# The recurrent branch's output weights read whole ahead of attention, and small DMAs issued by GpSimd

## Chip, cores and metric

The kernel runs on one core of one Trainium2 chip. The metric is device time of one execution in microseconds (us); lower is better. Times below are medians over runs; the trace is of one profiled execution. Engines: TensorE (PE, with its weight loads PEld), VectorE (DVE), ScalarE (ACT), GpSimd (POOL), SyncE (SP). An ending q (ACTq, SPq, POOLq) marks DMA issues by that engine's sequencer.

## The reference

One layer of a hybrid block on 1024 tokens of width 1024, in float32. An input projection feeds three dilated-window attentions (12 heads), a recurrent branch (RWKV, 8 heads of 64) and two gates; both branches are projected to the model's width, gated and added; an output projection and a mixture of 32 experts follow.

```python
h = rms_norm(x, norm1_gain)
p = h @ w_in
q, k, v, p_rwkv, p_gate = jnp.split(p, [...], axis=-1)
...
for g, (win, dil) in enumerate(ATT_PATTERNS):
    o_g, l_g = dilated_window_attention(q[:, :, g], k[:, :, g], v[:, :, g], ..., win, dil)
...
wts = jax.nn.softmax(jnp.stack(lses, axis=0), axis=0)
att = jnp.einsum('gbsh,gbshe->bshe', wts, jnp.stack(outs, axis=0).astype(jnp.float32))
y_att = att.reshape(B, S, ATT_OUT_WIDTH).astype(x.dtype) @ w_att_out
y_rwkv = rwkv7_time_mix(p_rwkv, ..., w_rwkv_out)          # ends with o @ w_rwkv_out
gates = jax.nn.sigmoid(p_gate.astype(jnp.float32)).astype(x.dtype)
mixed = gates[..., :D] * y_att + gates[..., D:] * y_rwkv
x = x + mixed @ w_out
x = x + hierarchical_moe(rms_norm(x, norm2_gain), ...)    # 32 experts, 2 per token
```

## The kernel before

Every float32 product is made of three fp32r matmuls: an operand is split into a high part (ACT copies it to fp32r) and a low part (DVE subtracts), by `split`, and `mm3` adds high x high, high x low and low x high in PSUM. The stages follow one another: input projection and RWKV preparation (0 to 410 us of the trace), the RWKV scan (to about 550), attention (about 573 to 921), the two branch projections (to 1022), output projection and router (to 1140), experts (1160 to the end). In the scan and in attention the remaining input-projection matmuls (line L307) fill PE; the last of them end at 932.

The order on each engine is set by a scheduler when the kernel is built: it takes the code's order, but moves an instruction according to when its operands and its buffer are free. Buffers come from pools; a pool opened where a closed one lay gets its memory when the last user of the old one is done. A DMA is issued by the engine it is written for and waits in that engine's queue, ahead of what stands behind it: for its source, for its buffer, and for the previous transfer that used the same one of eight completion semaphores of its kind (DMAHW for ACT and SP, DMASW for POOL).

The branch stage. `ohi`/`olo` are the split recurrent output. `load_wr(n)` reads a 128-column slice of `w_rwkv_out` (256 KB, rows of 512 bytes) and splits it into `wrh`/`wrl`; for each n two PSUM tiles are made with 12 matmuls each (L1090 through `mm3`), gated with `ga` into `mix`. Beside it 4 MB of `w_out` are read and split (`woh`, `wol`) for the later output projection. `MLc` holds the maxima and sums of the three windows' softmaxes; 12 small instructions turn them into mixing weights `wgt`, which are stored to `dWG` and read back broadcast over 64 partitions (`wb`, 256 KB each, 12 loads). For each of two head pairs three window outputs `og` are multiplied with `wb` and added; the third product is POOL's (L1187). The sums are split into `ahi`/`alo`, the attention output weights `w_att_out` are read by SP in two tiles and split, and 96 matmuls, gated with 16 more `ga` tiles, are added to `mix`.

The output projection. `mixsplit(i)` splits the 128 tokens `mix[:, i]` into `mxh` and a low part; the first two are written ahead of the loop, and the scheduler sets their place. Their `mxh` come from the pool `pmx`. Constants for norm and router (`g2`, `wr36`, `g2c`, `br36`, `rc`) are loaded on ACT's queue, and a block of zeros, `zpad`, is stored to the output's spare rows. Expert weights (512 KB pieces) are prefetched by SP into a list of areas; the first five are the pool `mr2`, then six of `mr`, then parts of `mix`.

```python
    for i in range(NRAW2):
        load_raw(N0 + i)
    ...
    def mixsplit(i):
        mh = pmx.tile([128, 8, 128], F32R, name="mxh")
        if i < 2:
            ml = raw4k().bitcast(F32R).rearrange("q (n t) -> q n t", t=128)
        ...
        split(mh, ml, mix[:, i])
```

## Time and profile before

| | before |
|---|---|
| median of 3 runs | 1787.5 us |
| lowest, highest | 1787.35, 1788.68 us |
| span of the profiled execution | 1787.2 us |
| own time of the profiled execution | not recorded beside the span |
| mean granted TensorE clock | 0.968 |
| PE, DVE, ACT, POOL busy | 94%, 71%, 49%, 26% of the span |
| DMA | 363.44 MB, mean 203 GB/s |

The span runs from the first to the last instruction. Shares are means over stages with different limits; for the change only the stretch from 920 to 1040 us matters directly, and the rows further down are of it and of two stretches used for prices.

### The profile page before, as it was taken

The page shows a single profiled execution, that of the slowest core. Times are in us where ns is not written, and L with a number is a line of the kernel's source. Part 1 is how long each engine was busy: PE and PEld are TensorE (multiplying, and loading weights), DVE is VectorE, ACT ScalarE, POOL GpSimd, SP SyncE. Part 2 cuts the span into 40 slices and gives each one's busy share as a digit, 9 for nine tenths or more (in the row PEclk, how much of TensorE's full clock was granted, in tenths as well). Part 3 has the DMA queues.
Part 4 walks back from the last instruction along what each step waited for, and adds up shares of the span by engine and source line. Part 5 has one row for each costly group of instructions (what it writes and reads, how often), then busy time and mean ns, then how long its engine had stood idle before and what let it go on. Part 6 is the DMA issues. An engine that isn't in the chain of part 4 may idle for free. (4 is left out here: it accounts for less than half of the span.)

```text
span 1787.2 us, 25862 instructions
## 1 busy us (share of the span) xinstructions
PE 1680.3 (94%) x9395; PEld 1325.3 (74%) x9396; DVE 1263.4 (71%) x2122; ACT 873.7 (49%) x1315; POOL 461.6 (26%) x380
## 2 busy tenths in 40 slices
PE   8999999999999999999998999699998999899996
PEld 6677777777777777777766777588777877777884
DVE  5647788783664444444436666689999999999985
ACT  4523434422221333344342122388777888777774
POOL 0110112223431000000100311234455455444431
PEclk9998989998999999999999999799999999999998
DMA  8323223363662110111249773699999999999991
GB/s 285 138 69 133 92 92 116 136 241 119 219 198 80 33 45 30 48 40 51 101 145 259 220 288 130 220 307 362 358 349 309 378 343 382 356 354 360 373 348 28
DMA packets 145619, 363.44 MB, mean 203 GB/s; under 512 B 17316, under 2 KB 62772, under 8 KB 145484
## 3 DMA queue, kind: packets, MB, share of 16 engines
q1 hardware_dynamic: 123108, 303.67, 47.4%
q0 software_dynamic: 15872, 50.35, 10.1%
q10 hardware_dynamic: 6504, 7.69, 1.6%
q8 instruction: 76, 1.25, 0.3%
q14 instruction: 59, 0.48, 0.1%
HBM read 307.49 MB, written 62.29 MB: 207 GB/s over the span
## 5 line engine op out<-in xcount | busy, mean ns | idle before, releaser
L1531 PE MATMUL pb<-u,xTh 128*128 128x512 f32 x1024 | 338.4, 406 | 1.2 <-ACT xTh L1526 1.2
L307 PE MATMUL pa<-xlo,wh 128*128 128x512 f32 x736 | 307.7, 418 | 0.0
L307 PE MATMUL pa<-xhi,wl 128*128 128x512 f32 x736 | 302.1, 411 | 2.3 <-DVE wl L278 2.3
L307 PE MATMUL pa<-xhi,wh 128*128 128x512 f32 x736 | 301.7, 410 | 1.5 <-DVE raw L427 1.0
L1417 DVE TENSOR_TENSOR u<-raw,u 128x1024 fp32r<-128x1024 f32 x182 | 297.5, 1676 | 5.5 <-ACT u L1415 5.3
L1415 ACT ACTIVATE u<-raw 128x1024 fp32r<-128x1024 f32 x216 | 224.3, 1056 | 47.5 <-PE pb L1531 28.8
L1531 PE MATMUL pb<-u,xTl 128*128 128x512 f32 x512 | 209.2, 409 | 21.1 <-DVE xTl L1527 21.1
L1531 PEld LDWEIGHTS pb<-u,xTh 128*128 128x128 f32 x1024 | 191.3, 189 | 40.7 <-ACT xTh L1526 2.0
L307 PEld LDWEIGHTS pa<-xlo,wh 128*128 128x128 f32 x736 | 141.1, 192 | 40.6 <-issue 11.0
L307 PEld LDWEIGHTS pa<-xhi,wh 128*128 128x128 f32 x736 | 141.4, 192 | 34.5 <-issue 2.9
L307 PEld LDWEIGHTS pa<-xhi,wl 128*128 128x128 f32 x736 | 141.6, 192 | 34.1 <-DVE wl L278 3.2
L1417 DVE TENSOR_TENSOR u<-mix,u 128x1024 fp32r<-128x1024 f32 x108 | 162.2, 1538 | 4.4 <-ACT u L1415 4.4
L1531 PE MATMUL pa<-u,hTh 128*128 128x512 f32 x512 | 146.0, 406 | 5.5 <-POOL u L1417 4.6
L1415 ACT ACTIVATE u<-mix 128x1024 fp32r<-128x1024 f32 x128 | 133.6, 1057 | 23.1 <-PE pb L1531 15.8
L1531 PEld LDWEIGHTS pb<-u,xTl 128*128 128x128 f32 x512 | 96.8, 189 | 45.0 <-DVE xTl L1527 27.9
L978 DVE SCALAR_TENSOR_TENSOR Sb<-pb,rqk,bias 128x128 f32<-128x128 f32 (+1 forms) x96 | 35.5, 406 | 124.5 <-PE pb L977 116.6
L1510 POOL DMA_INDIRECT out<-row,tba x30 | 62.6, 2086 | 219.4 <-ACT u L1415 56.5
L1531 PEld LDWEIGHTS pa<-u,hTh 128*128 128x128 f32 x512 | 94.6, 191 | 28.2 <-POOL u L1417 5.5
L1417 POOL TENSOR_TENSOR u<-raw,u 128x1024 fp32r<-128x1024 f32 x34 | 101.3, 2980 | 47.2 <-ACT u L1415 41.6
L276 ACT ACTIVATE wh<-wr 128x1024 fp32r<-128x1024 f32 x49 | 51.8, 1057 | 113.9 <-PE pa L307 90.1
L1531 PE MATMUL pa<-u,hTl 128*128 128x512 f32 x256 | 81.6, 400 | 1.2 <-DVE hTl L1527 1.2
L982 ACT ACTIVATE Sb<-Sb,ML 128x128 f32<-128x128 f32 (+1 forms) x96 | 42.3, 442 | 54.7 <-DVE ML L980 54.7
(419 smaller groups left out, 3014.4 us busy)
## 6 DMA issues: line engine op xcount, KB each, us to landing
raw<-in_w_expert_up SPq DMA_DIRECT2D x72, 512.0 KB
raw<-in_w_expert_gate SPq DMA_DIRECT2D x71, 512.0 KB
raw<-in_w_expert_down SPq DMA_DIRECT2D x71, 512.0 KB
wr<-in_w_in SPq DMA_DIRECT2D x49, 512.0 KB
mix<-in_w_expert_down SPq DMA_DIRECT2D x46, 512.0 KB
mix<-in_w_expert_gate SPq DMA_DIRECT2D x42, 512.0 KB
mix<-in_w_expert_up SPq DMA_DIRECT2D x40, 512.0 KB
dGA<-gs POOLq DMA_DIRECT2D x32, 256.0 KB, 3.6
```

Of the source, the lines that this page charges most:

```text
L276: nc.scalar.activation(wh, wr, AF.Copy)
L307: nc.tensor.matmul(ps, a[:, k, :], b[:, k, hs], start=(n == 0), stop=(n == 23))
L978: nc.vector.scalar_tensor_tensor(Sb[:, hh, 0:nk], pS[:, 0:nk], u.rn[:, 0, i, hh:hh + 1], u.bias[:, hh, 256 - nk:], op0=ALU.mult, op1=ALU.add)
L982: nc.scalar.activation(Sb[:, hh, 0:nk], Sb[:, hh, 0:nk], AF.Exp, bias=u.ML[:, i, hh:hh + 1], accum_out=u.ML[:, i, 2 + hh:3 + hh])
L1415: nc.scalar.activation(hi, raw, AF.Copy)
L1417: en.tensor_tensor(lo, raw, hi.bitcast(F32), op=ALU.subtract)
L1510: nc.gpsimd.indirect_dma_start(out=out, out_offset=bass.IndirectOffsetOnAxis(ap=idx, axis=0), in_=src, in_offset=None, compute_op=ALU.add)
L1531: nc.tensor.matmul(ps, x, w, start=first, stop=last)
```

## The change

`w_rwkv_out` is read whole into one tile `wrk` (16 KB per partition) by one SP DMA, written ahead of attention; the eight `load_wr` then only split slices of it. 24 small DMAs (8 loads of `MLc`, 4 stores of `dWG`, 12 broadcast loads of `wb`) are issued by POOL, not by ACT. The tile's pool `wk` stays open: its four slices of 4 KB take the place of four of the five `mr2` buffers as first areas for expert weights. The pool `pmx` is opened after the branch stage's pools are closed, not ahead of them. Removed comment lines are left out of the diff.

```diff
+    s9 = ctx.enter_context(ExitStack())
+    wk = s9.enter_context(tc.tile_pool(name="wk", bufs=1, reuse_waits="tile"))
+    wrk = wk.tile([128, 4, D], F32, name="wrk")
+    nc.sync.dma_start(wrk, I["w_rwkv_out"].rearrange("(k p) n -> p k n", p=128))
     s3 = ExitStack()
     pq = s3.enter_context(tc.tile_pool(name="pq", bufs=2, reuse_waits="tile"))
...
-    s9 = ctx.enter_context(ExitStack())
     mr = s9.enter_context(tc.tile_pool(name="mr", bufs=NRAW, reuse_waits="tile"))
...
-    pmx = s9.enter_context(tc.tile_pool(name="pmx", bufs=2, reuse_waits="tile"))
     s6 = ExitStack()
...
-            nc.scalar.dma_start(ML[32 * h:32 * h + 32, a], dML[a, h].rearrange("g (b t) -> b g t", t=32))
+            nc.gpsimd.dma_start(ML[32 * h:32 * h + 32, a], dML[a, h].rearrange("g (b t) -> b g t", t=32))
...
-        nc.scalar.dma_start(dWG[h].rearrange("g (b t) -> b g t", t=32), wg[32 * h:32 * h + 32])
+        nc.gpsimd.dma_start(dWG[h].rearrange("g (b t) -> b g t", t=32), wg[32 * h:32 * h + 32])
...
     def load_wr(n):
-        wr = p7.tile([128, 4, 128], F32, name="wr")
-        nc.sync.dma_start(wr, wrv[:, :, 128 * n:128 * n + 128])
         wh = p7.tile([128, 4, 128], F32R, name="wrh")
         wl = p7.tile([128, 4, 128], F32R, name="wrl")
-        split(wh, wl, wr)
+        split(wh, wl, wrk[:, :, 128 * n:128 * n + 128])
...
-                nc.scalar.dma_start(wb[hrs[hh]], dWG[2 * hp + hh, g:g + 1].to_broadcast([64, S]))
+                nc.gpsimd.dma_start(wb[hrs[hh]], dWG[2 * hp + hh, g:g + 1].to_broadcast([64, S]))
...
     s7.close()
     s6.close()
+    pmx = s9.enter_context(tc.tile_pool(name="pmx", bufs=2, reuse_waits="tile"))
...
-    mr2 = s9.enter_context(tc.tile_pool(name="mr2", bufs=NRAW2, reuse_waits="tile"))
-    areas = ["mr2"] * NRAW2 + ["mr"] * NRAW + list(range(8)) + ["mx"] * 2 + ["ph"] * NPH
+    mr2 = s9.enter_context(tc.tile_pool(name="mr2", bufs=NRAW2 - 4, reuse_waits="tile"))
+    areas = [("wk", a) for a in range(4)] + ["mr2"] * (NRAW2 - 4) + ["mr"] * NRAW + list(range(8)) + ["mx"] * 2 + ["ph"] * NPH
...
+        elif isinstance(area, tuple):
+            raw = wrk[:, area[1]]
```

Three places show how the order changes. A row names the line, the operation and its tiles with buffer numbers, and the semaphores that it waits for: DMAHW and DMASW are transfers, the others engines. Line numbers differ by one to three between the two kernels (L1081 is L1084).

First, ACT in the branch stage of the kernel before, from the first broadcast load on.

```order
L1186 DMA raw_8355<-dWG_76 64x1024 [waits DMAHW4_49,DMAHW0_49,DVE_49]
L1186 DMA raw_8355<-dWG_76 64x1024 [waits DMAHW6_49]
L1186 DMA raw_8361<-dWG_76 64x1024 [waits DMAHW5_49,DVE_49,Activation_49]
L1081 ACTIVATE wrh_8135<-wr_8133 128x512 [waits PE_49]
L1186 DMA raw_8361<-dWG_76 64x1024 [waits DMAHW0_49]
L1186 DMA raw_8368<-dWG_76 64x1024 [waits DMAHW3_49,DVE_49]
L1186 DMA raw_8368<-dWG_76 64x1024 [waits DMAHW5_49]
L1081 ACTIVATE wrh_8179<-wr_8177 128x512 [waits DMAHW4_49,PE_49]
L1186 DMA raw_8377<-dWG_76 64x1024 [waits DMAHW7_49,DMAHW0_49,DVE_49]
L1186 DMA raw_8377<-dWG_76 64x1024 [waits DMAHW2_49]
L1186 DMA raw_8383<-dWG_76 64x1024 [waits DMAHW4_49,DMAHW5_49,DMAHW3_49,Pool_49]
L1081 ACTIVATE wrh_8223<-wr_8221 128x512 [waits PE_49,Activation_49]
```

The same place of the changed kernel, from the fourth split of the recurrent weights on.

```order
L1084 ACTIVATE wrh_8085<-wrk_5012 128x512 [waits PE_49]
L1084 ACTIVATE woh0_8009<-raw_8257 128x512 [waits DMAHW1_49]
L1084 ACTIVATE woh1_8007<-raw_8257 128x512
L1084 ACTIVATE woh0_8009<-raw_8295 128x512 [waits DMAHW4_49]
L1084 ACTIVATE woh1_8007<-raw_8295 128x512
L1084 ACTIVATE woh0_8009<-raw_8333 128x512 [waits DMAHW6_49]
L1084 ACTIVATE woh1_8007<-raw_8333 128x512
L1084 ACTIVATE wrh_8127<-wrk_5012 128x512 [waits DVE_49,PE_49]
L1084 ACTIVATE wrh_8169<-wrk_5012 128x512 [waits DVE_49,PE_49]
L1084 ACTIVATE wrh_8211<-wrk_5012 128x512 [waits DVE_49,PE_49]
L1084 ACTIVATE ahi_7888<-raw_8339 128x1024 [waits DVE_49]
L1084 ACTIVATE wrh_8253<-wrk_5012 128x512 [waits PE_49,Activation_49]
```

The broadcast loads between the splits are gone, and the four last `wrh` follow the splits of `w_out` without a DMA among them; none of the `wrh` waits for a transfer.

Second, POOL in the kernel before, from the last stores of gates (`dGA`) to the first additions into `mix`.

```order
L384 DMA dGA_79<-gs_7808 128x512 [waits DMASW4_49,Activation_49]
L384 DMA dGA_79<-gs_7848 128x512 [waits DMASW5_49,Activation_49]
L384 DMA dGA_79<-gs_7966 128x512 [waits DMASW6_49,Activation_49]
L384 DMA dGA_79<-gs_7995 128x512 [waits DMASW7_49,Activation_49]
L1187 TENSOR_TENSOR raw_8366<-raw_8366,raw_8368 128x1024 [waits DMAHW3_49,DMAHW2_49,DMAHW5_49,DVE_49,DMAHW7_49,PE_49,Activation_49]
L1187 TENSOR_TENSOR raw_8388<-raw_8388,raw_8390 128x1024 [waits DMAHW3_49,DMAHW6_49,DMAHW1_49,DVE_49]
L1214 TENSOR_TENSOR mix_8005<-mix_8005,ga_8422 128x4x128 [waits DVE_49]
L1214 TENSOR_TENSOR mix_8005<-mix_8005,ohig_8409 128x4x128 [waits DVE_49] x4
```

POOL in the changed kernel, ahead of the same additions; the eight loads of `MLc` and the four stores of `dWG` stand above these rows.

```order
L1185 DMA raw_8347<-dWG_76 64x1024 [waits DMAHW1_49,DMAHW5_49,DMASW6_49,DVE_49]
L1185 DMA raw_8347<-dWG_76 64x1024 [waits DMASW7_49]
L1185 DMA raw_8354<-dWG_76 64x1024 [waits DMAHW2_49,DMAHW6_49,DVE_49,Activation_49]
L1185 DMA raw_8354<-dWG_76 64x1024
L1185 DMA raw_8363<-dWG_76 64x1024 [waits DMASW6_49,DMASW7_49,DMASW2_49,DVE_49]
L1186 TENSOR_TENSOR raw_8352<-raw_8352,raw_8354 128x1024 [waits DMAHW4_49,DMASW1_49,DMASW0_49]
L1185 DMA raw_8363<-dWG_76 64x1024 [waits DMASW3_49]
L1185 DMA raw_8369<-dWG_76 64x1024 [waits DMASW4_49,Pool_49]
L1185 DMA raw_8369<-dWG_76 64x1024 [waits DMASW5_49]
L1185 DMA raw_8376<-dWG_76 64x1024 [waits DVE_49]
L1185 DMA raw_8376<-dWG_76 64x1024
L1186 TENSOR_TENSOR raw_8374<-raw_8374,raw_8376 128x1024 [waits DMAHW2_49,DMASW7_49,DMASW6_49]
```

The broadcast loads stand on POOL, ten of the 12 in these rows; its first multiplication is behind seven of them, the second behind all 12.

Third, ACT at the start of the output projection, before, from the last split of the attention weights on.

```order
L1081 ACTIVATE raw_8405<-raw_8398 128x1024 [waits DMAHW7_49,Pool_49]
L1081 ACTIVATE mxh_8625<-mix_8005 128x1024 [waits Pool_49]
L1081 ACTIVATE mxh_8632<-mix_8005 128x1024
L1339 DMA g2_8592<-in_g2 128x1024 [waits DMAHW4_49,PE_49,Activation_49]
L1341 DMA wr36_8594<-in_w_rt 128x8x36 [waits DMAHW6_49]
L1343 DMA g2c_8596<-in_g2c 128x8 [waits DMAHW7_49]
L1346 DMA br36_8599<-in_b_rt 128x36 [waits DMAHW1_49,Pool_49]
L1348 DMA rc_8601<-in_rc 128x208 [waits DMAHW2_49]
L1355 DMA out_0<-zpad_8590 1024x1x128 [waits DMAHW3_49,Pool_49]
```

The same place after the change.

```order
L1084 ACTIVATE raw_8391<-raw_8384 128x1024 [waits DMASW6_49,DMASW7_49,DMASW3_49,DMAHW2_49,DMASW2_49,Activation_49]
L1341 DMA g2_8581<-in_g2 128x1024 [waits DMAHW5_49,Pool_49]
L1343 DMA wr36_8583<-in_w_rt 128x8x36 [waits DMAHW7_49,PE_49,Activation_49]
L1345 DMA g2c_8585<-in_g2c 128x8 [waits DMAHW1_49]
L1348 DMA br36_8588<-in_b_rt 128x36 [waits DMAHW2_49]
L1350 DMA rc_8590<-in_rc 128x208 [waits DMAHW4_49]
L1357 DMA out_0<-zpad_8579 1024x1x128 [waits DMAHW5_49,Pool_49]
L1084 ACTIVATE mxh_8610<-mix_8003 128x1024
L1084 ACTIVATE mxh_8617<-mix_8003 128x1024
```

The two `mxh` now stand behind the constants' loads and the store of `zpad`. In the changed kernel `g2` waits for POOL's last addition into `mix`, and `zpad` for the transfer of `g2` (DMAHW5 in both rows); before, `mxh` waited only for POOL's additions into the tokens concerned. On DVE the two low parts (`raw` from `mix` and `mxh`) moved from among the attention branch's gating to behind the product of `wr36` and `g2c`.

## Rows read from the trace of the kernel before

**Rows 1.** The page's busy us, share of the span and instructions, of TensorE.

```profile
PE 1680.3 (94%) x9395; PEld 1325.3 (74%) x9396; DVE 1263.4 (71%) x2122; ACT 873.7 (49%) x1315; POOL 461.6 (26%) x380
```

**Rows 2.** Windows: length, busy us by engine, granted clock, DMA share, GB/s.

```profile
960.00:980.00 20.00, 15.04 (x55) 10.72 (x53) 7.89 (x9) 2.32 (x3) 2.37 (x1) 0.91 1.06 276
1020.00:1040.00 20.00, 19.98 (x99) 16.19 (x98) 10.73 (x32) 3.76 (x9) 6.71 (x9) 1.00 0.94 342
```

**Rows 3.** PE's timeline: start, us, what, and idle time before, with releaser.

```profile
936.54 0.79 PE L1090 MATMUL pa<-ohi,wrh 128*128 128x512 f32 x1 [4.40 <-ACT wrh L1081]
...
937.63 0.80 PE L1090 MATMUL pa<-ohi,wrl 128*128 128x512 f32 x1
...
982.47 0.80 PE L1090 MATMUL pa<-ohi,wrl 128*128 128x512 f32 x1 [3.25 <-DVE wrl L1082]
...
999.58 1.22 PE L1090 MATMUL pa<-ahi,raw 128*128 128x512 f32 x2 [0.53 <-DVE raw L1082]
...
1022.17 0.40 PE L1090 MATMUL pa<-woh,mxh 128*128 128x512 f32 x1
```

**Rows 4.** Windows of 2.5 us after the stop at 936, same columns.

```profile
937.50:940.00 2.50, 2.50 (x7) 1.89 (x7) 1.98 (x7) 0.83 (x2) 0.54 (x1) 0.50 0.95 340
940.00:942.50 2.50, 2.50 (x10) 2.01 (x9) 0.49 (x1) 0.12 (x1) 0.00 (x0) 0.70 0.93 281
```

**Rows 5.** ACT's timeline; ACTq rows are DMA issues by its sequencer.

```profile
930.95 4.86 ACTq L1110 DMA_DIRECT2D MLc<-dML  x5
...
959.71 5.55 ACTq L1186 DMA_DIRECT2D raw<-dWG  x3
...
968.77 8.22 ACTq L1186 DMA_DIRECT2D raw<-dWG  x3
...
977.10 0.63 ACT L1081 ACTIVATE wrh<-wr 128x512 fp32r<-128x512 f32 x1 [11.11 <-DMA ga<-dGA]
...
997.21 1.06 ACT L1081 ACTIVATE raw<-raw 128x1024 fp32r<-128x1024 f32 x1 [1.22 <-DMA raw<-in_w_att_out]
...
1013.34 2.02 ACT L1081 ACTIVATE mxh<-mix 128x1024 fp32r<-128x1024 f32 x2 [15.06 <-POOL mix L1214]
...
1026.64 0.64 ACTq L1355 DMA_DIRECT2D out<-zpad  x1
```

**Rows 6.** POOL's timeline, same columns.

```profile
938.62 0.54 POOL L384 DMA_DIRECT2D dGA<-gs  x1 [9.82 <-ACT gs L383]
...
974.15 2.37 POOL L1187 TENSOR_TENSOR raw<-raw 128x1024 f32<-128x1024 f32 x1 [34.99 <-DMA raw<-dWG]
...
991.24 2.40 POOL L1187 TENSOR_TENSOR raw<-raw 128x1024 f32<-128x1024 f32 x1 [14.73 <-DMA raw<-dWG]
...
1023.53 1.29 POOL L1214 TENSOR_TENSOR mix<-mix,olog 128x512 f32<-128x512 f32 x1 [1.23 <-DVE olog L1213]
```

**Rows 7.** Window of 20 us in the scan stage, columns as in group 2.

```profile
420.00:440.00 20.00, 20.00 (x233) 15.97 (x234) 3.82 (x8) 4.50 (x9) 7.41 (x14) 0.85 0.35 113
```

**Rows 8.** DMA view of 950 to 990: packets, and the first queue.

```profile
DMA packets 5539, 10.66 MB, mean 267 GB/s; under 512 B 528, under 2 KB 2576, under 8 KB 5538
...
q1 hardware_dynamic: 4580, 7.51, 72.7%
```

**Rows 9.** DMA view of 1180 to 1220, in the expert stage.

```profile
DMA packets 3942, 14.20 MB, mean 355 GB/s; under 512 B 481, under 2 KB 481, under 8 KB 3938
...
q1 hardware_dynamic: 3549, 12.93, 87.8%
```

**Rows 10.** SP's timeline: two DMA issues.

```profile
993.66 0.33 SPq L1198 DMA_DIRECT2D raw<-in_w_att_out  x1
...
1024.85 0.33 SPq L1333 DMA_DIRECT2D xt<-in_x  x1
```

**Rows 11.** DVE's timeline: a split's low part, and the first use of `xt`.

```profile
1014.57 1.22 DVE L1082 TENSOR_TENSOR raw<-mix,mxh 128x1024 fp32r<-128x1024 f32 x1
...
1030.52 0.69 DVE L1462 SCALAR_TENSOR_TENSOR xt<-pa,xt 128x512 f32<-128x512 f32 x1 [5.27 <-DMA xt<-in_x]
```

More of the change, by code (lines that the diff above doesn't have):

```diff
@@ L1122, in block_kernel @@
     for h in range(4):
-        nc.scalar.dma_start(dWG[h].rearrange("g (b t) -> b g t", t=32), wg[32 * h:32 * h + 32])
+        nc.gpsimd.dma_start(dWG[h].rearrange("g (b t) -> b g t", t=32), wg[32 * h:32 * h + 32])
     wav = I["w_att_out"].rearrange("(k p) n -> p k n", p=128)
-    wrv = I["w_rwkv_out"].rearrange("(k p) n -> p k n", p=128)
     wrs = {}
     def load_wr(n):
-        wr = p7.tile([128, 4, 128], F32, name="wr")
-        nc.sync.dma_start(wr, wrv[:, :, 128 * n:128 * n + 128])
         wh = p7.tile([128, 4, 128], F32R, name="wrh")
         wl = p7.tile([128, 4, 128], F32R, name="wrl")
-        split(wh, wl, wr)
+        split(wh, wl, wrk[:, :, 128 * n:128 * n + 128])
         wrs[n] = wh, wl
```

## The prediction

> **What bounds the kernel now.** I read the page's busy shares first: TensorE (PE) is busy for 94% of the span [rows 1], so a change pays only where PE stands still or runs slowly, or where it makes PE do so. Then the 20 us windows around the change [rows 2]. From 960 to 980 PE is busy for 15.04 of 20 us while the DMA share is 1.06, that is, all 16 DMA engines are occupied; from 1020 on it is full, on the output projection, at a clock of 1.00. So the branch stage can give time back, and the output projection, which has none to spare, loses whatever time it is made to wait.
>
> PE's timeline gives the stage's ends [rows 3]. The first branch matmul starts at 936.54 after 4.40 us of waiting for `wrh`; the first with `wrl`, two matmuls later, at 937.63. The seventh piece of weights is waited for 3.25 us, up to 982.47. The attention branch runs without a stop only from 999.58, when the low part of its second weight tile exists. At 1022.17 the output projection follows the last attention matmul with no wait in its row.
>
> Each stop is dearer than its idle time: after the one at 936.54 the clock stands at 0.50 and then at a mean of 0.70 [rows 4], so the lower of the two levels (1.2 GHz) holds till about 941.5, and half of these 5 us, some 2.2 to 2.5 us, is lost besides. (At 0.70, with 0.50 and 1.00 the two levels, 60% of that 2.5 us window is slow.)
>
> The reason for the late pieces is on ScalarE (ACT): its timeline shows DMA issues that hold its queue, because they wait for earlier transfers [rows 5]: 4.86 us for five `MLc` loads, 5.55 and 8.22 us for three broadcast loads each. The split of the seventh piece starts at 977.10, just behind the block of 8.22 us. GpSimd (POOL) meanwhile does nothing between 939 and 974 [rows 6].
>
> **Part 1: the weights are read whole, early.** One 2 MB load in the scan stage replaces eight of 256 KB. Its issue needs a wait on PE work already done, and no attention instruction gets a new wait; I set its cost there at nothing, because around its place, from 420 to 440, the DMA engines are occupied for 0.35 of the time [rows 7]. Without that cover it would delay whatever load it stands ahead of by about 2.1 MB / 355 GB/s = 5.9 us. What it takes out of the busy stretch can be bounded. From 950 to 990, 2576 packets are under 2 KB, 528 of them under 512 B [rows 8], and the 2048 between are four of the old loads (512 B rows). By bytes alone, 1.05 MB at the 355 GB/s of a later stretch [rows 9], they are 3.0 us. By the mean packet of their queue (72.7% of 16 x 40 us over 4580 packets = 102 ns) they are 2048 x 102 ns / 16 = 13 us. The queue's larger packets later took 87.8% of 640 us over 3549 = 158 ns for 3.6 KB each; at some 124 ns (an estimate between this and its share by bytes) for the other 2532 packets of 2.6 KB, 74 ns stay for each small one, and 9.5 us for the four loads. I take 9.5 of all-engine time.
>
> The Trainium skill ("DMA: Bandwidth & Descriptors", Specifications) puts the smallest transfer that runs at line rate at 512 B, by which the four loads would cost only the 3.0 us of their bytes. The trace speaks against it here: the stretch with the 512 B packets moved 267 GB/s with all engines occupied, the other 355.
>
> **Part 2: 24 small DMAs go from ACT's queue to POOL's.** On ACT this frees the splits. The first `wrh` no longer stands behind 4.86 us of `MLc` issues: it can run by the time PE becomes free, at 936.54 - 4.40 = 932.1. `wrl` on VectorE (DVE) still stands behind the two `mmin` instructions, which need the first `MLc` loads; POOL can issue them at about 929 to 931 (an estimate: ACT had issued its first three before the row at 930.95), so they land some 4 us later, at 933 to 935, and the first `wrl` matmul can start at 934.5 to 936, against 937.63: 2 to 3 us earlier. On POOL each issue costs about 0.54 us (the `dGA` row of [rows 6]), 24 of them 13 us, which fit into its idle 35 us before 974. But what stands behind them on POOL are its two multiplications.
>
> These set the end of the stage. The second multiplication, 991.24 to 993.64, frees the buffer into which SyncE (SP) loads the second attention weight tile; that load is issued at 993.66 [rows 10], ACT has it at 997.21 [rows 5], PE at 999.58. After the change the first multiplication can start once the third broadcast pair has landed: it was issued by 965.26 and used at 974.15, 8.9 us later in the saturated stretch. POOL, which has only the broadcasts to issue, can issue that pair at 957 to 960 (an estimate from the start of ACT's row at 959.71, before its 5.55 us), so I get 965 to 969, ending 967.5 to 971.5; then the last pairs are issued, which needs 2 to 3 us, land 5 to 9 us later, and the second multiplication ends at 979.5 to 984.5 instead of 993.64. The weight tile then takes 3.55 us, as now, to 6 us, because 1 MB of expert weights can now stand ahead of it, and the two splits 2.4 us as before. The attention branch starts without a stop at 985.5 to 993 instead of 999.58: 6.5 to 14 us earlier. PE's recurrent part can follow: its eighth piece no longer waits for a load. I take the middle, **gain A = 10.5 us** (the 2 to 3 us at the start are part of it: an earlier start only counts if the end is earlier).
>
> The Trainium skill (the same page, Issuing engines are not separate DMA queues) says that issuing on several engines saves only the sequencer's time, usually small beside the transfer, and its Specifications give a queue of POOL's kind 1 us to the first byte against 0.6 us for ACT's. By that alone, with nothing else counted, 24 transfers would be later by 0.4 us each and A near zero. The trace disagrees for this place: the sequencer's time here is the 4.86, 5.55 and 8.22 us that splits stood behind.
>
> **Part 3: `pmx` is opened after the stage's pools are closed.** This is no transfer, but it moves work, as the order shows: ACT's first two `mxh` instructions, which ran at 1013.34 in the middle of the attention branch, now stand behind the six constant DMAs, the last of which (`zpad`) waits for the landing of the first (`g2`), and `g2` waits for POOL's last addition. The output projection's first matmul needs `mxh`, its third `mxl`. With T the end of the last attention matmul (1022.2 in the trace): POOL's last addition ends at 1023.53 + 1.29 = 1024.82, T + 2.6. `g2` takes from 3.55 us (the attention weights, also 512 KB) to 5.67 us (`xt`, 512 KB, issued at 1024.85 [rows 10] and used at 1030.52 [rows 11]) to land, T + 6.2 to 8.3. Then `zpad` is issued (0.64 us), one `mxh` takes 1.0 us (two in 2.02 [rows 5]), `mxl` 1.22 us [rows 11]: the third matmul starts at T + 9.1 to 11.2 instead of two matmuls after T (some 0.45 us), so PE loses 8.6 to 10.7 us, and 2.2 us more for the slow clock after the stop. **Loss B = 12 us** (10.5 to 15; the upper end for a landing of 8 us, as in the saturated stretch). Nothing covers it: PE is full behind it [rows 2], and the router and the experts follow. Of the expert weights, four buffers are filled earlier, but the buffers are as many as before and full before the experts begin; I set this at nothing.
>
> **Sum.** -10.5 + 12 = +1.5 us. The profiled execution's span, 1787.2 us, is 0.3 below the median of 1787.5 and has no time of its own beside it, so I add to the median: **1789.0 us**.
>
> **Rivals.** (1) *The gain wins.* POOL's broadcasts land at once because the stretch is no longer saturated (9.5 us of DMA time less), in the 3.55 us of the attention weights; the second multiplication then ends at about 978 and A is 15.5. With `g2` landing in 3.55 us too, B = 10.5: 1782.5. It decides from A - B > 3.6 us on. For it speaks the 9.5 us; against it that all other loads of the stage remain: in [rows 8] the 2048 packets are under half of the 5539. (2) *The stop at the output projection wins; slower.* POOL's issue chain holds its own multiplications, because each broadcast waits for a landing on POOL's queue as it did on ACT's (5.55 us for three), and A stays at 6.5; `g2` lands late because SP's expert weights fill the engines (DMA share 0.94 in [rows 2]), and B is 13.5: 1794.5. It decides from B - A > 3.6 us on. (3) *The transfers were hidden anyway*: A near 2, if the attention weight load still comes when it came; with B = 12 that is 1797.5. It is unlikely: `wrl` waits of 3.25 us and 4.40 us at the start were exposed. (4) *The moved `mxh` is not late*: B near 0, if `g2` and `zpad` were issued before T; then 1777. Against it: `g2`'s area is freed by POOL's last addition, which comes after T.
>
> **Chances.** A measurement here tells no difference within 0.2%, that is 3.6 us: 1783.9 to 1791.1. My sum with its neighbourhood gets 0.42 (same); rival 1, with the little of rival 4 (0.03), 0.25 (faster); rivals 2 (0.27) and 3 (0.06) together 0.33 (slower). The range leaves out rival 4, most of rival 3 and the far ends of A and B: 1781 (A = 15.5, B = 9) to 1796.5 (A = 5.5, B = 14.5). The likeliest case's own range is 1785 to 1792.
>
> **What would show it.** Right: no L1131 loads of 256 KB, a 2 MB load near 425; ACT's `wrh` free of stops of 8 us; the attention branch's end at about 1011.7; and then, on PE's row of the first output-projection matmuls, waits for `mxh` and `mxl` of together 8 to 11 us with ACT's two `mxh` behind `zpad`, and a clock of 0.50 after them. Wrong, if those waits are under 5 us (B overrated), if the attention branch still ends after 1016 (A overrated), or if the expert stage's length changes by over 2 us, which I set at nothing.

## The result and the profile after

The changed kernel takes 1806.3 us (median of 20 runs, 1788.6 to 1819.6), the kernel before 1789.4 (20 runs in turn with it, 1778.1 to 1807.3). The ratio is 1.0083 [1.0061, 1.0105], which leaves disturbed runs out and so is not quite the quotient of the medians: **slower by some 14.9 us [10.9, 18.8]**. The forecast was 1789.0, range 1781 to 1796.5, "no difference" the likeliest.

Runs of one kernel lie up to 11 to 18 us from its median on either side, and they follow the mean granted clock (changed kernel: 1788.6 us at 0.978, 1801.1 at 0.967, 1819.6 at 0.959). Part of it falls long before the place of the change: the last matmul ahead of the branch stage (L307) ends at 932.0 in the profile of before and at 927.3 in that of after (its start plus 0.23 us, the usual step from one such matmul to the next). So stages are compared from there. The profiled execution of after took 1801.1 us, span 1799.3.

The page's busy us, as in [rows 1]: TensorE is busy for the same time within 3 us, while the span is 12 us longer.

```profile
PE 1677.3 (93%) x9395; PEld 1321.6 (73%) x9396; DVE 1267.7 (70%) x2122; ACT 874.3 (49%) x1315; POOL 464.8 (26%) x404
```

Windows of after (columns as in [rows 2]): the branch stage still has all DMA engines occupied (1.03) and PE busy for 16.82 of 20 us; the window of the output projection's start has 14.56 where before had 19.98, at a clock of 0.68.

```profile
960.00:980.00 20.00, 16.82 (x65) 12.73 (x63) 12.09 (x13) 2.21 (x3) 5.43 (x7) 0.91 1.03 268
...
1020.00:1040.00 20.00, 14.56 (x47) 11.12 (x48) 3.57 (x5) 2.73 (x4) 1.29 (x1) 0.68 0.75 251
```

PE's timeline of after, to be held against [rows 3]:

```profile
927.63 0.50 PE L1093 MATMUL pa<-ohi,wrh 128*128 128x512 f32 x1 [0.20 <-ACT wrh L1084]
...
932.03 0.80 PE L1093 MATMUL pa<-ohi,wrl 128*128 128x512 f32 x1 [3.20 <-DVE wrl L1085]
...
969.85 0.47 PE L1093 MATMUL pa<-ohi,wrh 128*128 128x512 f32 x1 [3.16 <-DVE mix L1171]
...
986.73 0.47 PE L1093 MATMUL pa<-ahi,raw 128*128 128x512 f32 x1 [2.87 <-DVE mix L1171]
...
1013.04 0.39 PE L1093 MATMUL pa<-ahi,raw 128*128 128x512 f32 x1
1023.18 0.79 PE L1093 MATMUL pa<-woh,mxh 128*128 128x512 f32 x1 [9.75 <-ACT mxh L1084]
1023.77 0.63 PE L1093 MATMUL pa<-wol,mxh 128*128 128x512 f32 x1
1026.66 0.79 PE L1093 MATMUL pa<-woh,raw 128*128 128x512 f32 x1 [2.26 <-DVE raw L1085]
...
1032.37 0.61 PE L1093 MATMUL pa<-woh,mxh 128*128 128x512 f32 x1
1032.80 0.42 PE L1093 MATMUL pa<-wol,mxh 128*128 128x512 f32 x1
```

The first `wrh` is no longer waited for (0.20 us instead of 4.40), but `wrl` now is (3.20 us), and the stage ends little earlier. The stops at 969.85 and 986.73, where the attention branch begins, are for `mix`, a gating on DVE. For the first of them DVE's timeline shows why it comes late:

```profile
967.88 1.23 DVE L1190 TENSOR_TENSOR raw<-raw 128x1024 f32<-128x1024 f32 x1 [4.26 <-POOL raw L1186]
969.02 0.68 DVE L1171 SCALAR_TENSOR_TENSOR mix<-ga,pa 128x512 f32<-128x512 f32 x1
```

The gating stands in DVE's queue behind an addition that waits 4.26 us for POOL's first multiplication. So in place of the weights' pieces, the gating now holds PE.

At the output projection stands what wasn't in [rows 3]: 9.75 us for `mxh`, 2.26 us for the low part, and a matmul every 0.43 us, that is the lower clock, until 1032.8.

Why `mxh` is late is in three views: POOL's last addition, ACT's queue behind it, and DVE.

```profile
1014.24 1.26 POOL L1213 TENSOR_TENSOR mix<-mix,olog 128x512 f32<-128x512 f32 x1 [1.43 <-DVE olog L1212]
```

```profile
1015.53 0.37 ACTq L1341 DMA_DIRECT2D g<-in_g  x1
...
1016.45 0.59 ACTq L1345 DMA_DIRECT2D g2c<-in_g2c  x1
...
1021.39 0.63 ACTq L1357 DMA_DIRECT2D out<-zpad  x1
1022.07 2.00 ACT L1084 ACTIVATE mxh<-mix 128x1024 fp32r<-128x1024 f32 x2 [33.57 <-DMA g<-in_g]
```

```profile
1025.01 0.46 DVE L1346 TENSOR_TENSOR wr<-wr,g2c 128x288 f32<-128x288 f32 x1 [10.55 <-DMA g2c<-in_g2c]
1025.39 2.35 DVE L1085 TENSOR_TENSOR raw<-mix,mxh 128x1024 fp32r<-128x1024 f32 x2
```

ACT's two `mxh` stand behind `zpad`, `zpad` waits for the landing of `g2` (shown as `g`; 5.86 us from its issue to `zpad`'s), and `g2` waits for the last addition, which ends at 1015.50. In [rows 5] the `mxh` ran at 1013.34, inside the attention branch. On DVE the low parts stand behind the product of `wr36` and `g2c`, and `g2c` lands only at 1025.0, 8.6 us after its issue.

To see where the whole difference lies I cut each profile into five stretches. They are bounded by the end of the last L307 matmul; T, the end of the last attention matmul (again its start plus 0.23 us); the start of the first output-projection matmul with a low part ("third" below); the first and the last expert matmul (L1531 in before, L1533 in after); and the end of the span. Rows marked "again" are second profiles of the same kernel; "one execution" marks kernels of which only the profiled execution was timed.

| profile | branch stage, to T | T to third | third to experts | experts | tail | ratio to before |
|---|---|---|---|---|---|---|
| before | 90.2 | 0.4 | 136.4 | 615.3 | 12.9 | |
| before, again | 88.8 | 0.5 | 136.5 | 614.8 | 13.2 | one execution |
| after | 86.0 | 13.4 | 139.2 | 618.1 | 15.3 | 1.0083 [1.0061, 1.0105] |
| after, again | 87.2 | 13.2 | 138.0 | 618.7 | 15.0 | one execution |
| e1_mxh_first | 87.2 | 3.4 | 138.7 | 617.4 | 15.1 | 1.0057 [1.0020, 1.0093] |
| e2_pmx_late_only | 85.3 | 11.2 | 139.2 | 616.2 | 13.3 | 1.0053 [1.0020, 1.0086] |
| e3_actq | 89.4 | 13.4 | 140.0 | 613.0 | 13.5 | 1.0073 [1.0035, 1.0112] |
| e4_poolq_only | 85.1 | 0.5 | 136.5 | 618.2 | 15.2 | 0.9997 [0.9965, 1.0029] |
| e5_mxh_in_wrk | 85.8 | 0.4 | 141.3 | 617.8 | 14.9 | 0.9970 [0.9939, 1.0000] |
| e9_wr36_early | 86.1 | 0.4 | 136.3 | 616.8 | 14.9 | 1.0012 [0.9982, 1.0042] |
| e10_wb_only | 87.7 | 0.5 | 136.5 | 617.0 | 14.3 | one execution |
| e11_zpad_sp | 86.7 | 11.6 | 138.2 | 617.3 | 14.8 | one execution |
| e12_half_ga | 80.9 | 13.4 | 138.9 | 619.0 | 15.2 | one execution |

After against before, by the means of their two profiles: branch stage -2.9, stop at the output projection +12.9, the stretch with the slow matmuls behind it +2.1, experts +3.3, tail +2.1: +17.5 us, against +14.9 [10.9, 18.8] timed.

### The profile page after: what moved, and what is told of

Its sections match the earlier page's. It is cut to its first block, busy times and chain, and to the rows that moved or that the text cites. A ratio compares the mean times of both kernels' runs of the same rounds, so it can differ in the third digit from the quotient of the medians.

```text
span 1799.3 us, 25865 instructions
## 1 busy us (share of the span) xinstructions
PE 1677.3 (93%) x9395; PEld 1321.6 (73%) x9396; DVE 1267.7 (70%) x2122; ACT 874.3 (49%) x1315; POOL 464.8 (26%) x404
## 5 line engine op out<-in xcount | busy, mean ns | idle before, releaser
L1533 PE MATMUL pb<-u,xTh 128*128 128x512 f32 x1024 | 338.2, 406 | 2.4 <-ACT xTh L1528 2.4
L307 PE MATMUL pa<-xlo,wh 128*128 128x512 f32 x736 | 307.3, 418 | 0.0
L307 PE MATMUL pa<-xhi,wl 128*128 128x512 f32 x736 | 301.7, 410 | 2.3 <-DVE wl L278 2.3
L307 PE MATMUL pa<-xhi,wh 128*128 128x512 f32 x736 | 301.8, 410 | 1.5 <-DVE raw L427 1.0
L1533 PE MATMUL pb<-u,xTl 128*128 128x512 f32 x512 | 209.5, 410 | 30.6 <-DVE xTl L1529 30.6
L1533 PEld LDWEIGHTS pb<-u,xTh 128*128 128x128 f32 x1024 | 191.0, 189 | 41.5 <-ACT xTh L1528 3.2
L1419 DVE TENSOR_TENSOR u<-raw,u 128x1024 fp32r<-128x1024 f32 x124 | 201.0, 1656 | 2.9 <-ACT u L1417 2.7
L1419 DVE TENSOR_TENSOR u<-mix,u 128x1024 fp32r<-128x1024 f32 x108 | 173.4, 1642 | 4.1 <-ACT u L1417 4.1
L307 PEld LDWEIGHTS pa<-xlo,wh 128*128 128x128 f32 x736 | 141.1, 192 | 40.6 <-issue 11.0
L1417 ACT ACTIVATE u<-raw 128x1024 fp32r<-128x1024 f32 x148 | 154.1, 1056 | 27.7 <-PE pb L1533 20.7
L307 PEld LDWEIGHTS pa<-xhi,wh 128*128 128x128 f32 x736 | 141.2, 192 | 34.5 <-issue 2.9
L307 PEld LDWEIGHTS pa<-xhi,wl 128*128 128x128 f32 x736 | 141.3, 192 | 34.1 <-DVE wl L278 3.2
L1533 PE MATMUL pa<-u,hTh 128*128 128x512 f32 x512 | 143.4, 401 | 0.9 <-ACT hTh L1528 0.9
L1533 PEld LDWEIGHTS pb<-u,xTl 128*128 128x128 f32 x512 | 96.7, 189 | 56.7 <-DVE xTl L1529 40.0
L1512 POOL DMA_INDIRECT out<-row,tba x30 | 51.9, 1729 | 239.8 <-issue 70.7
L1533 PEld LDWEIGHTS pa<-u,hTh 128*128 128x128 f32 x512 | 93.4, 188 | 22.6 <-ACT hTh L1528 1.5
L1419 DVE TENSOR_TENSOR u<-wrk,u 128x1024 fp32r<-128x1024 f32 x58 | 89.4, 1574 | 1.3 <-ACT u L1417 1.3
L1533 PE MATMUL pa<-u,hTl 128*128 128x512 f32 x256 | 80.7, 396 | 1.2 <-DVE hTl L1529 1.2
L1419 POOL TENSOR_TENSOR u<-raw,u 128x1024 fp32r<-128x1024 f32 x24 | 73.0, 3041 | 26.0 <-ACT u L1417 17.2
```

Of the source, the lines that this page charges most:

```text
L307: nc.tensor.matmul(ps, a[:, k, :], b[:, k, hs], start=(n == 0), stop=(n == 23))
L1417: nc.scalar.activation(hi, raw, AF.Copy)
L1419: en.tensor_tensor(lo, raw, hi.bitcast(F32), op=ALU.subtract)
L1512: nc.gpsimd.indirect_dma_start(out=out, out_offset=bass.IndirectOffsetOnAxis(ap=idx, axis=0), in_=src, in_offset=None, compute_op=ALU.add)
L1533: nc.tensor.matmul(ps, x, w, start=first, stop=last)
```

## The experiments

My theory after the result: the output projection's stop (B) comes from the place where `pmx` is opened alone and is the bulk of the loss; the gain (A) is small because the stretch stays bound by bytes. Its rivals: the whole load and the early expert weights cost by themselves, and the queue move loses later what it gains.

**Is it the line of `pmx`?** First the splits alone put back ahead of the constants' loads, in the changed kernel.

```diff
     load_x(0)
+    def mixsplit(i):
...
+    nxt = mixsplit(0)
+    nx1 = mixsplit(1)
     zpad = p8.tile([128, 128], F32, name="zpad", bufs=1)
```

> The changed kernel with the first two mixsplit calls written ahead of the constants' loads, so that ACT's order is again mxh, mxh, g2, ..., zpad, with pmx still opened late. Theory 1 (the late mxh is the whole loss: PE stood 9.75 and 2.26 us at the start of the output projection, and 2.8 us more at the lower clock): no wait over 1 us there, time 13 to 17 us under the changed kernel, that is 0 to 6 us under the kernel before (ratio 0.997 to 1.000). Theory 2 (the expert stage or the early load also costs some 5 us, and the late mxh only two thirds of the loss): the waits go too, but the ratio stays at 1.002 to 1.004.

Measured: 1801.5 us, ratio 1.0057 [1.0020, 1.0093]. PE's timeline of this kernel has two waits left, for the low part and for DVE's `xt`:

```profile
1028.57 0.50 PE L1093 MATMUL pa<-woh,raw 128*128 128x512 f32 x1 [1.64 <-DVE raw L1085]
...
1041.40 0.66 PE L1383 MATMUL pb<-ident,xt 128*128 128x128 f32 x4 [2.30 <-DVE xt L1466]
```

T to third goes from 13.4 to 3.4 us and the kernel is still slower, at a ratio above both expectations (1.000 and 1.004 at most), though its interval reaches the second: the stop before the third matmul is not all of it. Part of the rest is the wait for `xt`, and part are experts and tail (617.4 and 15.1).

Then the line alone in the kernel before, with its eight loads and ACT's queue.

```diff
-    pmx = s9.enter_context(tc.tile_pool(name="pmx", bufs=2, reuse_waits="tile"))
     s6 = ExitStack()
...
     s6.close()
+    pmx = s9.enter_context(tc.tile_pool(name="pmx", bufs=2, reuse_waits="tile"))
```

> The kernel before with only the line that opens pmx moved behind the branch stage. Theory 1: the same stop of 11 to 13 us at the first output-projection matmuls and some 2.5 us at the lower clock; 13 to 17 us over the kernel before (ratio 1.007 to 1.010). Theory 2: a stop of about 8 to 10 us, ratio 1.004 to 1.006, since in the kernel before no part of the loss comes from the early load or the expert buffers.

Measured: 1799.6 us, ratio 1.0053 [1.0020, 1.0086]. PE's timeline of this kernel:

```profile
1016.21 0.80 PE L1090 MATMUL pa<-woh,mxh 128*128 128x512 f32 x1 [6.25 <-ACT mxh L1081]
...
1021.00 0.80 PE L1090 MATMUL pa<-woh,raw 128*128 128x512 f32 x1 [3.57 <-DVE raw L1082]
```

One moved line, which issues nothing, reproduces the stop (6.25 + 3.57 us, T to third 11.2 us) and makes the kernel slower by about 9.5 us [3.6, 15.4].

**How much of the stop is the store of `zpad`?** It is issued by SP in place of ACT; one execution.

```diff
-    nc.scalar.dma_start(out[S:S + 128].rearrange("q (j c) -> q j c", j=8), zpad[...
+    nc.sync.dma_start(out[S:S + 128].rearrange("q (j c) -> q j c", j=8), zpad[...
```

> The changed kernel with the store of zpad issued by SP. If the wait for g2's landing, behind which mxh stood, is the main part of the stop: mxh starts 2 to 4 us earlier (the issue of rc was over 2 to 3 us ahead of zpad's), and the first output-projection matmul 6 to 8 us after the last attention matmul, not 9.75; the first matmul with a low part still waits for DVE, whose product of wr36 and g2c stands ahead, so its start moves less, by 0 to 3 us. If the late pool itself (the last additions into mix) set it, no change.

PE's timeline:

```profile
1029.26 0.80 PE L1093 MATMUL pa<-woh,mxh 128*128 128x512 f32 x1 [6.04 <-ACT mxh L1084]
...
1034.65 0.80 PE L1093 MATMUL pa<-woh,raw 128*128 128x512 f32 x1 [3.74 <-DVE raw L1085]
```

`mxh` comes 3.7 us sooner (6.04 against 9.75), and the low part takes half of it back: the third matmul starts at T + 11.6 instead of 13.4. The chain has two arms, ACT behind `zpad` and DVE behind `g2c`, and to shorten one exposes the other.

**Does the version without the stop gain?** The first two `mxh` live in `wrk`'s tile, which is free once the last piece is split; the expert weights that went there come one step later.

```diff
+    mx = wk.tile([128, 4, D], F32R, tag="wrk", name="mx")
...
-        mh = pmx.tile([128, 8, 128], F32R, name="mxh")
+        if i < 2:
+            mh = mx[:, i].rearrange("q (n t) -> q n t", t=128)
+        else:
+            mh = pmx.tile([128, 8, 128], F32R, name="mxh")
```

> The changed kernel with the first two mxh in the place of wrk, whose last reader is the eighth weight split, and not in the late pool; the expert areas in that place are filled after the second output-projection step. Both mxh and both low parts then stand inside the attention branch again, and wr36 times g2c behind the first xt. Theory 1 (the rest of e1's loss is what its order still left late: low part 1.64 us, xt 2.3 us): no stop at the output projection and none at the first xt transpose, branch stage 85 to 88 us, from the first output-projection matmul to the first expert matmul 136 to 138 us; ratio 0.995 to 1.000. Theory 2 (early load or expert areas cost by themselves): 3 to 8 us slower than before, with the expert stage or the scan stage longer.

Measured: 1790.7 us, ratio 0.9970 [0.9939, 1.0000]. No stop before the output projection is left, but one on DVE takes its place, here in DVE's timeline, and then one on PE.

```profile
1023.18 0.46 DVE L1346 TENSOR_TENSOR wr<-wr,g2c 128x288 f32<-128x288 f32 x1 [2.07 <-DMA g2c<-in_g2c]
```

```profile
1026.62 0.44 PE L1384 MATMUL pb<-ident,xt 128*128 128x128 f32 x2 [1.89 <-DVE xt L1469]
```

The stretch from third to experts is 141.3 us, 4.8 more than before. So next, on top of it, the weights of the router and `g2c` are loaded and multiplied early, in place of their loads among the constants.

```diff
     nc.sync.dma_start(wrk, I["w_rwkv_out"].rearrange("(k p) n -> p k n", p=128))
+    wr36 = wk.tile([128, 8, 36], F32, name="wr36", bufs=1)
+    nc.sync.dma_start(wr36, I["w_rt"].rearrange("(k p) n -> p k n", p=128))
+    g2c = wk.tile([128, 8], F32, name="g2c", bufs=1)
+    nc.sync.dma_start(g2c, I["g2c"])
+    nc.vector.tensor_tensor(wr36, wr36, g2c[:, :, None].to_broadcast([128, 8, 36]), op=ALU.mult)
```

> e5 with the router weights and their gain (wr36, g2c, 148 KB) loaded and multiplied early, behind the load of wrk. In e5 DVE stood 2.07 us for g2c with the second xt addition behind it, and PE 1.9 us for that, with a lower clock after. Expected: no wait of over 1 us on PE between the attention branch and the router's last step; from the first output-projection matmul to the first expert matmul 136 to 138 us (e5: 141.7); ratio to before 0.992 to 0.998 if the branch stage keeps its 85 to 87 us. If the early load costs in the scan stage, 0.998 to 1.003.

Measured: 1792.0 us, ratio 1.0012 [0.9982, 1.0042]. The step from the attention branch to the output projection on PE now has no wait, and the stretch is 136.3 us, as before.

```profile
1018.82 0.39 PE L1098 MATMUL pa<-ahi,raw 128*128 128x512 f32 x1
1019.05 0.40 PE L1098 MATMUL pa<-woh,mx 128*128 128x512 f32 x1
1019.28 0.40 PE L1098 MATMUL pa<-wol,mx 128*128 128x512 f32 x1
1019.51 0.40 PE L1098 MATMUL pa<-woh,raw 128*128 128x512 f32 x1
```

Without its stop the change is worth nothing that can be timed (both intervals hold 1, or end at it): the bulk of the loss is the stop's, and the gain of the stage is small or given back elsewhere. The rival by which the early load costs by itself has no support: e9, with the load, is at 1.0012, and e4 below, without it, at 0.9997. That the expert weights are read one step later in e5 and e9 was not tried alone.

**Which part moves the branch stage?** Once the changed kernel with the 24 DMAs back on ACT, once the kernel before with them on POOL (the same lines, the other way).

```diff
-            nc.scalar.dma_start(ML[32 * h:32 * h + 32, a], dML[a, h]...
+            nc.gpsimd.dma_start(ML[32 * h:32 * h + 32, a], dML[a, h]...
...
-        nc.scalar.dma_start(dWG[h]...
+        nc.gpsimd.dma_start(dWG[h]...
...
-                nc.scalar.dma_start(wb[hrs[hh]], dWG[2 * hp + hh, g:g + 1]...
+                nc.gpsimd.dma_start(wb[hrs[hh]], dWG[2 * hp + hh, g:g + 1]...
```

> The changed kernel with the 24 small DMAs back on ACT's queue: whole early load and late pmx alone. If the queue is what gave the 4.3 us by which the branch stage became shorter (85.8 against 90.1 us from the last input-projection matmul to the last attention matmul), the stage is 89 to 91 us and the time 3 to 5 us over the changed kernel (ratio to before 1.010 to 1.012). If the whole load gave it, the stage is 85 to 87 us and the time that of the changed kernel (1.008).

> The kernel before with only the 24 small DMAs moved to POOL's queue. If the queue gave the shorter branch stage: 85 to 87 us, and 3 to 5 us under the kernel before (ratio 0.997 to 0.998). If the whole load gave it: 89 to 91 us and no difference (within 0.2%). mxh stays ahead of the constants, so no stop at the output projection in either case.

Measured: e3 1801.1 us, 1.0073 [1.0035, 1.0112], stage 89.4 us; e4 1789.6 us, 0.9997 [0.9965, 1.0029], stage 85.1 us. The first `wrh` on PE's timeline, first e3, then e4:

```profile
945.17 0.79 PE L1093 MATMUL pa<-ohi,wrh 128*128 128x512 f32 x1 [5.55 <-ACT wrh L1084]
```

```profile
942.52 0.51 PE L1090 MATMUL pa<-ohi,wrh 128*128 128x512 f32 x1 [0.20 <-ACT wrh L1081]
...
947.54 0.79 PE L1090 MATMUL pa<-ohi,wrl 128*128 128x512 f32 x1 [3.82 <-DVE wrl L1082]
```

With ACT's queue the stop at the first `wrh` is there even with the whole load (5.55 us); with POOL's it is gone even with eight loads. The whole load by itself shortens nothing (89.4 against 90.2 and 88.8). But e2, on ACT's queue, has a stage of 85.3 us, 3.5 to 4.9 below before's two: either one profile of this stage is uncertain by that much, or the late `pmx` shortens it; e3, which has the late `pmx` too, speaks against the second. The mean of the four profiles on ACT's queue is 88.4, of the seven with all 24 DMAs on POOL's (after, its second profile, e1, e4, e5, e9, e11) 86.3: about 2 us, in the direction of the queue, and no more than that. The end of POOL's second multiplication, counted from the stage's start, separates the two groups better: 58.6 to 61.6 us on ACT's queue, 56.2 to 58.1 on POOL's, 3.4 us by the means. The totals do not follow: e3, expected at 1.010 or more if the queue gave the gain, is at 1.0073 with the shortest experts of the table, and e4, expected at 0.997 to 0.998, shows no difference.

A smaller dose, the 12 broadcasts alone on POOL, and the two kernels once more, one execution each:

> The kernel before with the 12 broadcast loads alone on POOL's queue; MLc and dWG stay on ACT. Branch stage: 85 to 87 us if the broadcasts' place is what shortened it, with the 4 to 5 us wait for the first wrh kept; 88 to 90 us if it was the first wrh. Expert stage: kernels with 24 more DMAs on POOL took 617 to 619 us in it and had no DMA issue of over 3 us on POOL; kernels without had two of 6.5 us and 613 to 616 us. If the number of descriptors that POOL has written sets where these long issues fall, they stand at other places here, or are one or none, and the length goes with their number.

> The kernel before once more, for a second profile: how much the stages differ between executions of one kernel. If the branch stage's length (90.2 us from the last input-projection matmul to the last attention matmul) is a property of the kernel, 89 to 91 us here; if executions differ by as much as the changed kernel did (86.0), anything from 85 to 91.

> The changed kernel once more: the stop at the first output-projection matmuls should again be 11 to 14 us and the branch stage 85 to 87 us, whatever the start of the stage is.

Measured: e10 1781.3 us, stage 87.7, between its two expectations; before again 1783.9; after again 1802.0. The second profiles repeat the first within 1.4 us in every stretch of the table.

**What bounds the stage now?** The broadcasts were replaced by loads that read 64 different rows (the mixing weights are left out, so later routing and the whole time are not comparable; only this stage is read).

```diff
-                nc.gpsimd.dma_start(wb[hrs[hh]], dWG[2 * hp + hh, g:g + 1].to_broadcast([64, S]))
+                nc.gpsimd.dma_start(wb[hrs[hh]], dOG[2 * g + hp, hrs[hh]])
```

> The changed kernel with the 12 broadcast loads replaced by loads of the same size and count that read 64 different rows of dOG (so the mixing weights are left out of the computation). In the changed kernel the stretch from 950 to 990 still moved 274 GB/s with the engines occupied, and these loads took 8.1 us to land. If reading one row 64 times is what slows them: landing below 5 us, over 320 GB/s there, branch stage 80 to 83 us. If the sum of the transfers is what takes the time: landing 7 to 9 us and 85 to 87 us, as in the changed kernel.

Then half of the recurrent branch's gate loads were left out (8 of 16, 2 MB; the second half of each gate is not the layer's).

```diff
-            ga = gate(1, n, h)
+            if h == 0:
+                ga = gate(1, n, h)
```

> The changed kernel with eight of the 16 gate loads of the recurrent branch left out (the second half of the tokens is gated with the first half's gates, so the result is not the layer's). 2 MB fewer in the branch stage. If the stage is bound by what the DMA engines move (about 265 GB/s from 950 to 990): 78 to 81 us instead of 86 to 87. If by the chain of broadcast, POOL's multiplication and the attention weights whatever the load: 84 to 87 us.

Measured: e8 stage 84.9 us, broadcasts landing in 9.2 us, 263 GB/s from 950 to 990; e12 stage 80.9 us, landing in 6.2 us. DMA view of 950 to 990, first after (to be held against [rows 8]), then e12:

```profile
DMA packets 3825, 10.98 MB, mean 274 GB/s; under 512 B 508, under 2 KB 508, under 8 KB 3824
...
q1 hardware_dynamic: 2871, 7.85, 65.7%
...
raw<-dWG POOLq DMA_DIRECT2D x10, 256.0 KB, 8.1
```

```profile
DMA packets 4039, 11.44 MB, mean 286 GB/s; under 512 B 521, under 2 KB 521, under 8 KB 4038
...
raw<-dWG POOLq DMA_DIRECT2D x10, 256.0 KB, 6.2
```

Another address pattern of the broadcasts changes the stage by 1 to 2 us, within a profile's uncertainty. With 2 MB of gates less to move the stage is 5.7 us shorter than the mean of after's two profiles, and 2.1 MB at 355 GB/s [rows 9] are 5.9 us. That would fit a stage that follows its bytes, but e5 and e9 do not: no expert weight is issued in their branch stages until the last 6.4 us, e5 moved 9.03 MB from 950 to 990 (226 GB/s, DMA share 0.87) against 10.98 and 10.19 in after's two profiles, and yet their stages are 85.8 and 86.1 us and POOL's second multiplication ends at 56.2 us of the stage in both, as in after. e12 also takes eight issues out of SP's queue, and its second multiplication ends at 52.8. So the gate loads do hold the stage; whether by their bytes or by their place in SP's queue is not shown.

## Why the prediction was wrong, point by point

**What held.** The 2 MB load is issued at 424.02 and no instruction's wait is put down to it. ACT's splits are free of the stop at the first `wrh`. The output projection stops for `mxh`, then for the low part, in the order forecast and at the lower clock, and e2 shows that the line of `pmx` alone does it. Part of what is hidden holds too: none of the runs shows a cost of the four expert buffers filled early.

**The term A was mis-sized: 10.5 forecast, 2.9 measured** (86.6 against 89.5, and 1.6 to 4.2 from profile to profile). The attention branch ends at 1013.3 in after, near the 1011.7 forecast, by luck: the stage began 4.7 us sooner, before the change acts; from before's start it would be 1018, past the forecast's own sign of a wrong A (1016). Two steps failed.

The first is the price, which is no term of the sum but stands behind the shorter landings and rival 1: "I take 9.5 of all-engine time" for the four 256 KB loads of 512 B rows. They are gone from the stretch (508 packets under 2 KB, not 2576), yet it moves 274 GB/s with the engines as full as before, 255 in the second profile, against 267 and 245 in before. e4, which keeps them, has 283 GB/s and the shortest stage of those on POOL's queue. So the traces show no sign that small packets kept the rate at 267. The Trainium skill ("DMA: Bandwidth & Descriptors", Specifications) puts line rate at 512 B and up, by which, as an estimate from their bytes at 355 GB/s, they cost 3.0 us; the traces agree better with that than with my rate per packet, which I got by laying one queue's occupied time on its packets. Expert weights came into the same stretch, 1.5 MB by SP's timeline of after. They are not what ate the gain: e5 and e9 have neither them nor the small packets there, with stages of 85.8 and 86.1 us.

```profile
976.18 0.33 SPq L1322 DMA_DIRECT2D wrk<-in_w_expert_gate  x1
976.56 0.42 SPq L1322 DMA_DIRECT2D wrk<-in_w_expert_up  x1
...
983.55 0.33 SPq L1197 DMA_DIRECT2D raw<-in_w_att_out  x1
...
986.99 0.43 SPq L1322 DMA_DIRECT2D wrk<-in_w_expert_gate  x1
```

The second, and the one that the sum rests on, is the chain on POOL: "the last pairs are issued, which needs 2 to 3 us, land 5 to 9 us later". POOL's timeline of after:

```profile
955.20 1.02 POOL L1185 DMA_DIRECT2D raw<-dWG  x2 [3.42 <-issue]
962.05 0.51 POOL L1185 DMA_DIRECT2D raw<-dWG  x1 [5.84 <-DVE raw L1186]
965.48 2.36 POOL L1186 TENSOR_TENSOR raw<-raw 128x1024 f32<-128x1024 f32 x1 [2.92 <-DMA raw<-dWG]
967.80 1.59 POOL L1185 DMA_DIRECT2D raw<-dWG  x3
971.74 1.02 POOL L1185 DMA_DIRECT2D raw<-dWG  x2 [2.36 <-DVE alo L1085]
981.12 2.40 POOL L1186 TENSOR_TENSOR raw<-raw 128x1024 f32<-128x1024 f32 x1 [8.36 <-DMA raw<-dWG]
```

From the start of the stage (927.3 here, 932.0 in before), the first multiplication starts 38.2 us later (42.2 in before, 33 to 37 forecast) and the second ends at 56.2 us (61.6 in before, 47.5 to 52.5 forecast). The issues wait for DVE to free their buffers (5.84 and 2.36 us), which ACT's queue had met too, and a landing still takes 8 us. The weight tile behind it took what was forecast (983.55 to ACT's split at 987.45, 3.9 us). The forecast had counted the queue and left out the buffers. By the means of the two profiles each, the second multiplication ends 4.5 us sooner than before, and so does the attention branch start (59.8 against 64.3 us of the stage). The step from there to the stage's end failed too: the forecast carried the gain through whole, but the attention branch takes 26.8 us instead of 25.2, at a mean granted clock of 0.87 in both profiles (0.93 in before's), behind a stop of 2.87 us for `mix` in after. At the stage's start only the releaser changed: `wrl` is waited for where `wrh` was, and its first matmul starts 4.7 us into the stage (5.6 in before, 2.5 to 4 forecast).

On the Trainium skill's rule that several issuing engines save only the sequencer's time (the same page, Issuing engines are not separate DMA queues): the sequencer's time is real here (4.40 and 5.55 us at the first `wrh` against 0.20), but of it only some 2 us reach the end of the stage. That is nearer to the rule than to my 10.5. A later landing by POOL's queue is not clear of the spread: 8.1 and 9.3 us in after's two profiles, 8.4 by ACT's in before's second.

**The term B was mis-sized less: 12 forecast (10.5 to 15), 15.0 measured** (12.9 up to the third matmul, 2.1 behind it). I had put `mxl` one split behind `mxh`; in DVE's order the product with `g2c` stands between, which the order of the instructions had shown, and `g2c`, issued behind 512 KB of `g2`, landed 8.6 us after its issue. The wait for `g2` itself was 5.86 us, just above the 3.55 to 5.67 taken. For the clock, the 14 steps from 1026.66 to 1032.80 take 6.14 us, where 14 usual ones of 0.23 are 3.2: 2.9 us, 2.2 taken.

**"I set this at nothing" failed for the experts.** Experts and tail are 3.3 and 2.1 us longer; the text named over 2 us as a sign of being wrong. The early buffers are not the reason: e3 has them, on ACT's queue, with 613.0 and 13.5. In the table the length goes with POOL's queue; that this is the cause is not shown (the last section).

**The rivals.** Nearest came rival 2 in its effect (the stop wins, slower), with A = 2.9 below its 6.5 and B = 15.0 above its 13.5, and its condition on POOL is near what the rows show (issues that hold the multiplications, though for buffers and not for landings); B - A = 12.1 is far past its point of 3.6. For A it was rival 3's number (near 2), but not its reason: the weight load did come earlier, by about 5 us (56.2 against 61.7 us of the stage). 12.1 plus the 5.4 of experts and tail is the 17.5 of the profiles.

## What to carry to other kernels

When a buffer is opened later, ask which instructions first need it, and what stands ahead of them on every engine once they move: one line without a transfer cost more here than the transfers won. A block on one engine's queue is worth what is left when the next waiter (here DVE's buffers, the landing, `wrl`) has taken its place, not the block's own length. Occupied DMA engines do not make every removed byte count: here 2 MB of gate loads were worth 5.7 us, 1.5 MB of expert weights none that shows, so ask whether the chain that ends the stage waits for the load that you remove.

## What the hardware showed that I had not expected

**POOL's late indirect DMAs.** Among the 30 stores of expert rows (`out<-row`), which take POOL some 1.7 us each, two take 6.5 us in the kernel before, by its POOL timeline; in the kernel with 12 more DMAs on POOL (e10, second fence) it is one; with 24 more, none.

```profile
1373.42 6.59 POOL L1510 DMA_INDIRECT out<-row,tba  x1 [10.63 <-ACT u L1415]
...
1450.25 6.48 POOL L1510 DMA_INDIRECT out<-row,tba  x1 [8.44 <-DMA raw<-in_w_expert_up]
```

```profile
1303.76 6.52 POOL L1510 DMA_INDIRECT out<-row,tba  x1 [10.69 <-issue]
```

The two long ones are in every profile without the extra POOL DMAs (before twice, e2, e3: experts 613.0 to 616.2 us, tail 12.9 to 13.5), and in none of those with 24 (616.8 to 619.0, tail 14.8 to 15.3). e10, with one, has 617.0 and 14.3. So the kernels that lose the long instructions are the slower ones in this stage, and e4's 4.4 us from its branch stage are gone in its total. The last store, too, ends later after its issue (first before, then after; the span ends at 1787.2 and 1799.3, that is 10.9 and 13.4 us on):

```profile
1776.26 1.43 POOL L1510 DMA_INDIRECT out<-xin,tba  x1 [18.24 <-ACTq L1662]
```

```profile
1785.94 1.43 POOL L1512 DMA_INDIRECT out<-xin,tba  x1 [18.24 <-ACTq L1664]
```

This is a correlation over 13 profiles, with the edges (616.2 and 616.8) close together. Why some issues are long, and by what path their absence would cost 2 to 3 us, stays open; so does the use of POOL's queue with its own buffers for the broadcasts, which was not tried.

**The clock before the change.** The granted clock ahead of the branch stage differs from run to run (0.85 in [rows 7]; between 0.83 and 1.00 over the profiles from 300 to 400), and the start of the branch stage, between 923 and 942 us whatever the kernel, goes with it: up to 900 us the mean clock is 0.98 in e2 and e10, which start earliest, and 0.95 in e4, which starts last. That is more than the effect studied. Single spans could not have told these kernels apart; the table by stages and the timed ratios could.
